# Opening loads in one queue, more idle products in the first norm, no GpSimd arithmetic, and handed-on rows in a spread layout

## The chip, the cores and the metric

The kernel runs on one core of a Trainium2 chip. The metric is the device time of one execution in microseconds, the median of several runs. Three runs of the kernel before gave 3027.7, 3023.4 and 3025.57 us, so its time is 3025.57 us.

A core has these engines: TensorE (PE; its weight loads are shown apart as PEld), VectorE (DVE), ScalarE (ACT), GpSimd (POOL) and SyncE (SP, which here only issues transfers). Sixteen DMA engines move the data between memory and the core's buffers.

## The reference, cut to what matters

The program is one step of a decoder trunk with two layers, for a prompt of 256 tokens and a sample group of 8 sequences of 4 tokens, with 2048 features, all in float32. Each layer does, in this order:

```
x = x + mixer(rmsnorm(x));  x = x + convffn(rmsnorm(x))
x = x + sigmoid(rmsnorm(x) @ Wg) * (p @ Wp)
```

The mixer of layer 0 is causal pooling in four groups of 512 features, with windows w of 2, 4, 8 and 16 tokens: `d = mean(h over the last w tokens) - h`, then `d @ pool_w[group]`, times a scale. For the sample group the window reaches back into `state_pool`, the last 15 normalised rows of each sequence. The mixer of layer 1 is retention.

What the change touches, besides the opening of layer 0, are two of the outputs: the new pooling states. For the prompt they are the last 15 normalised rows (`h[241:256]`); for each sample sequence, the old rows 4 to 14 and the four new normalised rows.

## The kernel before, in words

All large products have 288 moving columns: 256 prompt tokens and 32 sample tokens, features on the partitions. A product in float32 precision is made of three products of split operands (`three`, lines 265 to 267: high by high, low by high, high by low). The weights come in pieces of 256 rows by 512 columns. For each piece, `dma` (line 1396) loads it on SP's queue into one of five buffers (`RAW_BUFS`), `split_hi` (line 1402) rounds it on ACT, and `split_lo` (line 1410) subtracts on DVE. A piece is used by 24 products. Pieces are split two ahead of their use, and the load of piece i+5 is issued when piece i's buffer has been read by `split_lo`.

The order of every engine's instructions is written out by the program itself: the product stream is emitted tile by tile, and between two tiles (`tick`) single operations from two lists, `main` and `side`, are emitted when an estimate of the engines' clocks says that their inputs are there. An engine executes its own instructions in the order of emission.

The opening (`PoolPhase`) has this order:

- `loads` issues the transfers. On SP's queue: the two halves of `x0` (prompt tokens 0 to 127) and of `x1` (128 to 255), with the identity and the four parts of `x4` (the sample's rows in a layout of four times 32 partitions) between them, then `pc`, `gbc`, `sb`, `pq`, and the first five weight pieces. On POOL's queue: `prow` (the norm weights, five loads), `sbb` (state rows for window 16) and a second copy of `gbc` for 32 other partitions.
- `start` squares the tokens' features on ACT (lines 403 and 405), transposes x to features on partitions on PE (`xT`, line 262), and works out the factor of the norm, one number per token (`rms_r`, a chain of twelve tiny DVE operations). While that runs, PE makes eight products of ones by ones, whose result is not used (line 422). In float32 each of these is two instructions.
- The pooling itself is a product: `x0`, `x1` and `sb` are the weights and small matrices `pq` and `pc` are the moving operand, which hold the window's shares. `weigh` (lines 470 and 471) multiplies `pq` by the token's norm factor, and `sbg` (line 476) multiplies the sample's rows by the norm weight. `quad` makes the four feature tiles of a group: three or four products each in a PSUM bank (lines 487 to 494; line 489 adds what the first 128 tokens give to the next ones, 2 to 16 columns wide), then `high` on ACT (498, 499) and `low` on DVE (502, 504). There are three such PSUM banks.
- `start` makes quads 0 and 1 before the first weight piece; quad 2 stands before group 1's pieces (each group has two), quad 3 before group 2's.
- `last` makes the handed-on rows with GpSimd arithmetic on 32 partitions by 2048 features: lines 513 and 514 for the prompt, line 516 for the sample, and three transfers from POOL's queue. Its place in the program is before group 2, but POOL starts each operation as soon as its inputs are there.

`FfnPhase.start` then opens the next phase.

## Time and profile before

| What | Value |
|---|---|
| Median of three runs | 3025.57 us (3023.4 to 3027.7) |
| Span of the profiled execution, first to last instruction | 3020.6 us |
| PE busy | 2998.1 us (99%) |
| DVE busy | 1963.7 us (65%) |
| ACT busy | 1416.2 us (47%) |
| POOL busy | 96.0 us (3%) |
| HBM traffic | 178 GB/s over the span |

The profile gives the profiled execution by its span of 3020.6 us alone. What lies around the span is not shown; the median of the three runs is 4.97 us above it. Start times in the rows are microseconds from the start of the span. `PE mm` is a product into one of the five large PSUM tiles, `PE ms` one into one of the three small ones.

### The profile page before, as it was taken

How to read it: one execution, taken by the hardware profiler on the slowest of the kernel's cores; microseconds unless marked ns; L12 is line 12 of the kernel's file. 1: busy time of each engine (PE TensorE's matmuls, PEld its weight loads, DVE VectorE, ACT ScalarE, POOL GpSimd, SP SyncE). 2: the span in 40 equal slices, each digit the busy share in tenths (PEclk: the TensorE clock that was granted, in tenths of full speed). 3: DMA queues.
4: the chain of work that ended last, by engine and by line, in shares of the span. 5: the costliest groups of instructions: out<-in, count | busy, mean ns of one | idle time of the engine just before them, and what ended most of it. 6: DMA issues, size and time to landing. Idle time of an engine off the chain costs nothing.

```text
span 3020.6 us, 54260 instructions
## 1 busy us (share of the span) xinstructions
PE 2998.1 (99%) x22019; PEld 2945.6 (98%) x22019; DVE 1963.7 (65%) x3396; ACT 1416.2 (47%) x2144; POOL 96.0 (3%) x131
## 2 busy tenths in 40 slices
PE   8999999999999999999999999999999999999998
PEld 8999999999999999999999999999999999999998
DVE  6666756565656767766766767676666565656565
ACT  4544434343444555445444444455444343434454
POOL 3000000000000000000000000000000000000000
PEclk8999999999999999999999999999999999999999
DMA  5655555555555566765766657566555555555543
GB/s 173 176 167 163 165 168 161 168 164 167 166 174 163 167 201 218 238 209 180 237 196 219 221 176 233 191 199 182 163 167 162 167 165 167 164 168 161 178 158 116
DMA packets 287906, 541.81 MB, mean 179 GB/s; under 512 B 18553, under 2 KB 55001, under 8 KB 287465
## 3 DMA queue, kind: packets, MB, share of 16 engines
q1 hardware_dynamic: 274968, 495.44, 53.5%
q0 software_dynamic: 12688, 42.91, 4.2%
q8 instruction: 173, 2.83, 0.4%
q14 instruction: 77, 0.63, 0.1%
HBM read 496.15 MB, written 42.84 MB: 178 GB/s over the span
## 4 chain that ended last, share of the span: by engine, by line
PE 98%; DVE 0%; DMA 0%; ACT 0%; issue 0%; SPq 0%; ACTq 0%
PE mm L265 31%; PE mm L267 30%; PE mm L266 30%; PE ms L262 1%; PE ms L1241 1%; PE ms L1225 1%; PE ms L1242 1%; PE ms L266 0%; PE ms L267 0%; PE ms L265 0%; DMA x<-in_x_prompt 0%; PE ms L1057 0%; PE ms L487 0%; PE ms L491 0%; PE ms L488 0%
## 5 line engine op out<-in xcount | busy, mean ns | idle before, releaser
L1402 ACT CAST hi<-raw 128x1024 fp32r<-128x1024 f32 x864 | 907.1, 1050 | 1393.0 <-PE mm L266 1185.1
L265 PE MATMUL mm<-xh,hi 128*128 128x288 f32 x4928 | 1465.2, 297 | 0.1
L266 PE MATMUL mm<-xl,hi 128*128 128x288 f32 x4928 | 1454.5, 295 | 0.0
L267 PE MATMUL mm<-xh,lo 128*128 128x288 f32 x4928 | 1449.7, 294 | 0.0
L1410 DVE TENSOR_TENSOR lo<-raw,hi 128x1024 fp32r<-128x1024 f32 x864 | 1054.4, 1221 | 552.0 <-ACT hi L1402 550.3
L265 PEld LDWEIGHTS mm<-xh,hi 128*128 128x128 f32 x4928 | 924.5, 188 | 12.1 <-DVE x L532 0.3
L266 PEld LDWEIGHTS mm<-xl,hi 128*128 128x128 f32 x4928 | 925.9, 188 | 4.7
L267 PEld LDWEIGHTS mm<-xh,lo 128*128 128x128 f32 x4928 | 928.4, 188 | 0.0
L266 PE MATMUL mm<-hl,hi 128*128 128x288 f32 x1408 | 415.4, 295 | 0.0
L267 PE MATMUL mm<-hh,lo 128*128 128x288 f32 x1408 | 415.1, 295 | 0.0
L265 PE MATMUL mm<-hh,hi 128*128 128x288 f32 x1408 | 413.3, 294 | 0.0
L265 PEld LDWEIGHTS mm<-hh,hi 128*128 128x128 f32 x1408 | 264.7, 188 | 0.0
L266 PEld LDWEIGHTS mm<-hl,hi 128*128 128x128 f32 x1408 | 264.7, 188 | 0.0
L267 PEld LDWEIGHTS mm<-hh,lo 128*128 128x128 f32 x1408 | 264.5, 188 | 0.0
L632 DVE SCALAR_TENSOR_TENSOR c<-U,cv,c 128x304 f32<-128x304 f32 x352 | 179.4, 529 | 3.5 <-ACT c L629 0.4
L265 PE MATMUL mm<-rhh,hi 128*128 128x288 f32 x512 | 152.2, 297 | 0.0
L267 PE MATMUL mm<-rhh,lo 128*128 128x288 f32 x512 | 151.5, 296 | 0.0
L266 PE MATMUL mm<-rhl,hi 128*128 128x288 f32 x512 | 149.8, 293 | 0.4 <-DVE rhl L1319 0.4
L722 DVE TENSOR_TENSOR x<-x,mm 128x288 f32<-128x288 f32 x192 | 82.5, 450 | 86.5 <-PE mm L267 86.5
L604 DVE TENSOR_TENSOR U<-mm,rb 128x256 f32<-128x256 f32 x176 | 73.7, 419 | 94.8 <-PE mm L267 94.8
L629 ACT ACTIVATE c<-U,cv 128x304 f32<-128x304 f32 x176 | 107.6, 635 | 15.4 <-DVE U L605 15.4
L1229 DVE SCALAR_TENSOR_TENSOR S<-S,ms 128x512 f32<-128x512 f32 x128 | 87.0, 681 | 37.0 <-PE ms L1225 36.8
(265 smaller groups left out, 2154.9 us busy)
## 6 DMA issues: line engine op xcount, KB each, us to landing
raw<-in_ffn_w_up SPq DMA_DIRECT2D x352, 512.0 KB
raw<-in_ffn_w_down SPq DMA_DIRECT2D x176, 512.0 KB
raw<-in_ret_w_in SPq DMA_DIRECT2D x128, 512.0 KB
raw<-in_ple_w_gate SPq DMA_DIRECT2D x64, 512.0 KB
raw<-in_ret_w_in SPq DMA_DIRECT2D x128, 256.0 KB
S<-in_state_ret SPq DMA_DIRECT2D x64, 512.0 KB
out_ret_s<-S POOLq DMA_DIRECT2D x64, 512.0 KB, 4.2
raw<-in_ret_w_out SPq DMA_DIRECT2D x64, 512.0 KB
```

The source lines that it names most:

```text
L262: T.transpose(out, in_, ident[:rows, :rows])
L265: T.matmul(out, w[0], a[0], start=start, stop=False)
L266: T.matmul(out, w[0], a[1], start=False, stop=False)
L267: T.matmul(out, w[1], a[0], start=False, stop=stop)
L604: V.tensor_tensor(U[:, s, 2:258], ps[:, 0:256], rb[:, 0:256], MUL)
L629: A.activation(c[0][:, 0:304], u[:, 2:306], AF.Identity, bias=w(3), scale=w(2))
L632: V.scalar_tensor_tensor(c[0][:, 0:304], u[:, s:304 + s], w(s), c[0][:, 0:304], MUL, ADD)
L722: V.tensor_tensor(x[:, M], x[:, M], ps[:, :NT], ADD)
L1225: T.matmul(ps, st["km", b][:, 128 * kk:128 * kk + 128], self.vst, start=True, stop=True)
L1229: V.scalar_tensor_tensor(s[:, kk], s[:, kk], g ** 4, st["u", b, kk], MUL, ADD)
L1402: A.copy(h, raw[i])
L1410: V.tensor_tensor(l, r, h.bitcast(F32), SUB)
```

## The change

1. Loads: `x1`'s first half is issued right behind `x0`'s second, then the four parts of `x4` and `pc`, then `x1`'s second half. Behind it come `pq` of group 0, `sb`, `gbc`, and the state rows of group 0 alone (112 KB instead of 336 KB), then the rest, two weight pieces, `pq` of groups 2 and 3, `sbb`, and three weight pieces. `sbb` and `gbc` leave POOL's queue (the second copy of `gbc` is gone); `prow` stays there. After the fifth piece, 21 small loads are added on SP's queue: a selection matrix `sel`, and the rows `xe`, `ge`, `g4` for point 4.
2. Norm: the transposed first half of `x1` is copied on DVE instead of ACT, the chain of tiny DVE operations is emitted ahead of the last two transposes, 16 idle products instead of 8, and the copy of the sample's x moves behind the first `sbg`.
3. Pooling products: `pq` is 272 columns per group instead of 384. The product with `x0` is 144 columns wide and reaches 16 columns into the second 128 tokens; the product with `x1` adds to them. The narrow product of line 489 is gone. In group 3 the product with `sb` has 88 rows instead of 32, the added ones with zeros.
4. Handed-on rows: no GpSimd arithmetic. Two products with `sel` spread the norm factors over partitions, one DVE copy keeps them, two DVE operations make the rows (the prompt's 15 rows on 120 partitions by 256 features, the sample's on 128 by 512), and six transfers leave from POOL's queue. They are emitted from `main`, from group 1 on. `FfnPhase.start` waits in the program's order until they are emitted.

```diff
-    pq = np.zeros((128, 4, 384), f)
+    pq = np.zeros((128, 4, 272), f)
...
+    sel = np.zeros((128, 2, 128), f)
+    sel[:32, 0] = np.tile(np.eye(32), (1, 4))
+    for t in range(15):
+        sel[113 + t, 1, 8 * t:8 * t + 8] = 1
...
             for i, t in enumerate((self.x0, self.x1)):
                 for h in range(2):
                     c = slice(h * (D // 2), (h + 1) * (D // 2))
+                    if i == h == 1:
+                        for j in range(4):
+                            SP.dma_start(self.x4[32 * j:32 * j + 32], x4[j])
+                        SP.dma_start(self.pc, I["pc"])
                     SP.dma_start(t[:, c], xp[128 * i:128 * i + 128, c])
                     if i == h == 0:
                         SP.dma_start(ident, I["ident"])
-                    if i + h == 1:
-                        for j in range(2 * i, 2 * i + 2):
-                            SP.dma_start(self.x4[32 * j:32 * j + 32], x4[j])
-            SP.dma_start(self.pc, I["pc"])
-            SP.dma_start(self.gbc[0:32], g0.partition_broadcast(32))
-            SP.dma_start(self.sb[0:32], I["x_sample"].rearrange("b t d -> (b t) d"))
-            SP.dma_start(self.pq[:, 0], I["pq"][:, 0])
-            SP.dma_start(self.sb[32:88, 0:1536], I["state_pool"][0, :, 8:15, 0:1536])
...
+            SP.dma_start(self.pq[:, 0], I["pq"][:, 0])
+            SP.dma_start(self.sb[0:32], I["x_sample"].rearrange("b t d -> (b t) d"))
+            SP.dma_start(self.gbc, g0.partition_broadcast(32))
+            SP.dma_start(self.sb[32:88, 0:512], I["state_pool"][0, :, 8:15, 0:512])
             SP.dma_start(self.pq[:, 1], I["pq"][:, 1])
-            dma(0)
+            SP.dma_start(self.sb[32:88, 512:2048], I["state_pool"][0, :, 8:15, 512:2048])
+            for i in range(2):
+                dma(i)
             SP.dma_start(self.pq[:, 2:4], I["pq"][:, 2:4])
-            for i in range(1, RAW_BUFS):
+            SP.dma_start(self.sbb, I["state_pool"][0, :, :, 1536:2048])
+            for i in range(2, RAW_BUFS):
                 dma(i)
-            GP.dma_start(self.sbb, I["state_pool"][0, :, :, 1536:2048])
-            GP.dma_start(self.gbc[96:128], g0.partition_broadcast(32))
+            SP.dma_start(self.sel, I["sel"])
+            SP.dma_start(self.xe, xp[241:256].rearrange("t (e c) -> (t e) c", e=8))
+            for t in range(15):
+                SP.dma_start(self.ge[8 * t:8 * t + 8], g0.rearrange("(e c) -> e c", e=8))
+            for j in range(4):
+                SP.dma_start(self.g4[32 * j:32 * j + 32], g0[512 * j:512 * j + 512].partition_broadcast(32))
...
-            self.xT(1, 0, False)
-            self.xT(1, 1, False)
+            self.xT(1, 0, True)
+            self.xT(1, 1, True)
...
+            V.tensor_tensor(ssq[:, 0:1], tiny[:, 9:10], tiny[:, 10:11], ADD)
+            V.tensor_copy(ssq[:32, 2:3], ps[:32, 0:1])
+            V.tensor_tensor(ssq[:, 1:2], tiny[:, 11:12], tiny[:, 12:13], ADD)
+            release(ps)
+            rms_r()
             self.xT(1, 2, False)
             self.xT(1, 3, False)
...
-            for _ in range(8):
+            for _ in range(16):
                 T.matmul(pw[:, 0:128], ones, ones, start=True, stop=True)
...
             self.direct(self.sbg(0))
+            A.copy(x[:, :, 256:288].rearrange("p (c j) t -> p c j t", j=4),
+                   px.rearrange("p (j c t) -> p c j t", j=4, c=4))
...
-                    T.matmul(ps[:, 0:128], self.x0[:, c], self.pq[:, gi, 0:128], start=True, stop=True)
-                    T.matmul(ps[:, 128:256], self.x1[:, c], self.pq[:, gi, 256:384], start=True, stop=False)
-                    T.matmul(ps[:, 128:128 + w], self.x0[:, c], self.pq[:, gi, 128:128 + w], start=False, stop=True)
+                    T.matmul(ps[:, 0:144], self.x0[:, c], self.pq[:, gi, 0:144], start=True, stop=True)
+                    T.matmul(ps[:, 128:256], self.x1[:, c], self.pq[:, gi, 144:272], start=False, stop=True,
+                             skip_group_check=True)
...
-                chains.append([op_(860 if gi < 3 else 1070, prod, nb=1), Op("A", 480, high), Op("V", 440, low)])
+                chains.append([op_(700 if gi < 3 else 850, prod, nb=1), Op("A", 480, high), Op("V", 440, low)])
...
         def last(self):
-            r = slice(96, 128)
-            GP.tensor_scalar(self.sqs[r], self.x1[r], rtok[r, 1:2], None, MUL)
-            GP.tensor_tensor(self.sqs[r], self.sqs[r], self.gbc[r], MUL)
-            GP.dma_start(O["pool_p"][0, 0], self.sqs[113:128])
-            GP.tensor_scalar(self.sb[0:32], self.sb[0:32], rtok[:32, 2:3], None, MUL)
-            GP.dma_start(O["pool_s"][0, :, 11:15, :], self.sb[0:32])
-            GP.dma_start(O["pool_s"][0, :, 0:11, :], I["state_pool"][0, :, 4:15, :])
+            c = {}
+            def factors():
+                ps = c[0] = sbank()
+                T.matmul(ps[:, 0:1], self.sel[:, 0], rtok[:, 2:3], start=True, stop=True)
+                T.matmul(ps[:, 1:2], self.sel[:, 1], rtok[:, 1:2], start=True, stop=True)
+            def keep():
+                V.tensor_copy(self.rsel, c[0][:, 0:2])
+                release(c[0])
+            def rows():
+                V.scalar_tensor_tensor(self.xe, self.xe, self.rsel[:120, 1:2], self.ge, MUL, MUL)
+                V.scalar_tensor_tensor(self.x4, self.x4, self.rsel[:, 0:1], self.g4, MUL, MUL)
+            def out():
+                GP.dma_start(O["pool_p"][0, 0].rearrange("t (e c) -> (t e) c", e=8), self.xe)
+                for j in range(4):
+                    GP.dma_start(O["pool_s"][0, :, 11:15, 512 * j:512 * j + 512], self.x4[32 * j:32 * j + 32])
+                GP.dma_start(O["pool_s"][0, :, 0:11, :], I["state_pool"][0, :, 4:15, :])
+                ready.add("rows")
+            main.extend(chained([op_(250, factors, nb=1), Op("V", 150, keep), Op("V", 900, rows)]) + [Op("N", 0, out)])
...
-                    if gi == 2:
+                    if gi == 1:
                         self.last()
...
-            force(lambda: not side)
+            force(lambda: not side and "rows" in ready)
```

## Rows read from the trace of the kernel before

**Rows 1.** Stretches: length, busy us (instructions) by engine, PE clock, DMA share, GB/s.

```profile
24.00:31.00 7.00, 5.74 (x27) 5.64 (x27) 5.70 (x7) 3.55 (x10) 6.24 (x3) 0.50 0.50 192
...
46.00:60.00 14.00, 14.00 (x113) 13.80 (x113) 10.79 (x27) 7.96 (x22) 0.00 (x0) 1.00 0.39 114
...
80.00:1000.00 920.00, 920.00 (x6920) 918.77 (x6919) 574.61 (x978) 420.23 (x601) 5.41 (x10) 1.00 0.56 167
```

**Rows 2.** Chain that ended last, in order of time: start, length, what.

```profile
4.81 10.77 DMA x<-in_x_prompt
...
19.88 4.06 DVE sb L476
...
26.33 0.59 PE ms L487 x2
...
38.00 0.40 PE mm L265
...
46.56 0.30 PE ms L487 x2
46.87 0.22 PE ms L488 x2
47.09 0.12 PE ms L489 x2
47.22 0.24 PE ms L491 x2
```

**Rows 3.** Waits of PE, first 60 us: total, times, longest.

```profile
PE ms L491 <- DVE sb L476: 2.2, 1, 2.2
...
PE ms L487 <- ACT xh L499: 1.3, 1, 1.3
```

**Rows 4.** Timeline of DVE and POOL: start, length, engine, line, operation.

```profile
19.56 5.57 POOL L513 TENSOR_SCALAR sqs<-x,rtok 32x2048 f32<-32x2048 f32 x1 [14.59 <-ACT x L429]
19.81 4.12 DVE L476 TENSOR_TENSOR sb<-sb,gbc 32x512 f32<-32x512 f32 x1
...
25.21 4.52 POOL L514 TENSOR_TENSOR sqs<-sqs,gbc 32x2048 f32<-32x2048 f32 x1
...
25.80 4.01 DVE L471 TENSOR_SCALAR pq<-pq,rtok 128x128 f32<-128x128 f32 x1
...
29.73 0.67 DVE L476 TENSOR_TENSOR sb<-sb,gbc 32x512 f32<-32x512 f32 x1
```

**Rows 5.** DMA: traffic of 2 to 16 us by queue; then stretches as in rows 1.

```profile
DMA packets 1455, 3.60 MB, mean 257 GB/s; under 512 B 300, under 2 KB 671, under 8 KB 1366
...
q0 software_dynamic: 288, 0.57, 17.7%
...
2.00:6.00 4.00, 1.03 (x5) 1.07 (x6) 0.00 (x0) 1.17 (x3) 2.97 (x6) 1.00 0.87 294
...
10.00:13.00 3.00, 1.97 (x8) 1.56 (x8) 0.56 (x2) 1.15 (x2) 0.00 (x0) 1.00 0.98 203
```

**Rows 6.** Timeline of PE: the idle products of line 422.

```profile
18.34 2.86 PE L422 MATMUL ms<-ones 128*128 128x128 f32 x16
```

**Rows 7.** Last stretches of PE alone: length, busy us (instructions), clock, DMA share, GB/s.

```profile
3006.80:3007.20 0.40, 0.40 (x4) 0.65 0.00 0
```

**Rows 8.** Groups by line, 22 to 45 us: count, busy us, mean ns of one.

```profile
L1410 DVE TENSOR_TENSOR lo<-raw,hi 128x1024 fp32r<-128x1024 f32 x4 | 4.9, 1214 | 0.0
...
L502 DVE SCALAR_TENSOR_TENSOR xl<-ms,par,xh 128x256 fp32r<-128x256 f32 x8 | 3.8, 476 | 4.1 <-ACT xh L499 4.1
...
L1402 ACT CAST hi<-raw 128x1024 fp32r<-128x1024 f32 x4 | 4.2, 1052 | 2.6 <-issue 2.6
...
L498 ACT ACTIVATE xh<-ms,par 128x256 fp32r<-128x256 f32 x8 | 3.8, 474 | 11.8 <-PE ms L491 11.8
```

**Rows 9.** Waits of SP's queue, first 60 us.

```profile
SPq L1396 <- DVE lo L1410: 32.5, 6, 12.1
...
SPq L392 <- DMA x<-in_x_prompt: 2.2, 1, 2.2
```

More of the change, by code (lines that the diff above doesn't have):

```diff
@@ L55, in _constants @@
             for j in range(max(0, t - win + 1), t + 1):
-                pq[j % 128, w, t + 128 * (j // 128)] += share
-            pq[t % 128, w, t + 128 * (t // 128)] -= 1
+                pq[j % 128, w, t + 16 * (j // 128)] += share
+            pq[t % 128, w, t + 16 * (t // 128)] -= 1
         for b in range(8):
@@ L70, in _constants @@
     c["pq"], c["pc"] = pq, pc
+    sel = np.zeros((128, 2, 128), f)
+    sel[:32, 0] = np.tile(np.eye(32), (1, 4))
+    for t in range(15):
+        sel[113 + t, 1, 8 * t:8 * t + 8] = 1
+    c["sel"] = sel
     half = DK // 2
@@ L367, in loads @@
             self.sb, self.sbb = t("sb", [128, D]), t("sbb", [120, 512])
-            self.pq, self.pc = t("pq", [128, 4, 384]), t("pc", [128, 6, 32])
-            self.prow, self.gbc, self.sqs = t("prow", [128, 128]), t("gbc", [128, D]), t("sqs", [128, D])
+            self.pq, self.pc = t("pq", [128, 4, 272]), t("pc", [128, 6, 32])
+            self.prow, self.gbc, self.sqs = t("prow", [128, 128]), t("gbc", [32, D]), t("sqs", [128, D // 2])
+            self.sel, self.rsel = t("sel", [128, 2, 128]), t("rsel", [128, 2])
+            self.xe, self.ge, self.g4 = t("xe", [120, 256]), t("ge", [120, 256]), t("g4", [128, 512])
             g0 = I["norm_mix"][0]
@@ L420, in start @@
             pw = sbank()
-            for _ in range(8):
+            for _ in range(16):
                 T.matmul(pw[:, 0:128], ones, ones, start=True, stop=True)
             release(pw)
-            V.tensor_tensor(ssq[:, 0:1], tiny[:, 9:10], tiny[:, 10:11], ADD)
-            V.tensor_copy(ssq[:32, 2:3], ps[:32, 0:1])
-            release(ps)
-            V.tensor_tensor(ssq[:, 1:2], tiny[:, 11:12], tiny[:, 12:13], ADD)
-            rms_r()
-            A.copy(x[:, :, 256:288].rearrange("p (c j) t -> p c j t", j=4),
-                   px.rearrange("p (j c t) -> p c j t", j=4, c=4))
             A.copy(par, pp[:, 0:128])
@@ L469, in weigh @@
             self.rdy = [
-                oa(256, lambda: A.activation(w[:, 0:256], w[:, 0:256], AF.Copy, scale=rtok[:, 0:1]), 1),
-                ov(128, lambda: V.tensor_scalar(w[:, 256:384], w[:, 256:384], rtok[:, 1:2], None, MUL))]
+                oa(144, lambda: A.activation(w[:, 0:144], w[:, 0:144], AF.Copy, scale=rtok[:, 0:1]), 1),
+                ov(128, lambda: V.tensor_scalar(w[:, 144:272], w[:, 144:272], rtok[:, 1:2], None, MUL))]
             return list(self.rdy)
@@ L485, in prod @@
                     ps = d[0] = sbank()
-                    w = WINDOWS[gi]
-                    T.matmul(ps[:, 0:128], self.x0[:, c], self.pq[:, gi, 0:128], start=True, stop=True)
-                    T.matmul(ps[:, 128:256], self.x1[:, c], self.pq[:, gi, 256:384], start=True, stop=False)
-                    T.matmul(ps[:, 128:128 + w], self.x0[:, c], self.pq[:, gi, 128:128 + w], start=False, stop=True)
+                    T.matmul(ps[:, 0:144], self.x0[:, c], self.pq[:, gi, 0:144], start=True, stop=True)
+                    T.matmul(ps[:, 128:256], self.x1[:, c], self.pq[:, gi, 144:272], start=False, stop=True,
+                             skip_group_check=True)
                     if gi < 3:
@@ L492, in prod @@
                     else:
-                        T.matmul(ps[:, 256:288], self.sb[:32, c], self.pc[:32, 3], start=True, stop=False)
+                        T.matmul(ps[:, 256:288], self.sb[:88, c], self.pc[:88, 3], start=True, stop=False)
                         T.matmul(ps[:, 256:288], self.sbb[:, 128 * (M - 12):128 * (M - 11)], self.pc[:120, 4],
```

## The prediction

> **What bounds the kernel now.** I read the table of stretches first. Once the work is under way TensorE is never idle: 920.00 us busy of the 920 from 80 to 1000 us [rows 1]. Whatever the change does to VectorE, ScalarE or GpSimd there costs nothing, and a microsecond is worth a microsecond only where TensorE waits or runs slowly. That is the opening, so I read the chain of waits over the first 60 us next. It shows three things [rows 2]. First, the second half of x1 is waited for from 4.81 to 15.58 us. Second, squares and the norm's chain take until 19.88, and there the sample's rows (line 476) hold the path for 4.06 us. Third, the pooling products follow, and the first weight product starts only at 38.00. The table of waits names the two holes that VectorE leaves in TensorE: 2.2 us before line 491 and 1.3 us before a line 487 [rows 3]. The timeline says why [rows 4]. The VectorE operation of line 476 that takes 4.12 us from 19.81 ran beside GpSimd's line 513 (19.56 to 25.13) and takes 0.67 us at 29.73. Line 471 took 4.01 us beside line 514 (25.21 to 29.73).
>
> The granted clock belongs to this. It is 0.50 (1.2 GHz) all through 24 to 31 us and 1.00 (2.4 GHz) from 46 to 60 [rows 1]. It had fallen after TensorE stood still for the 2.2 us, and a line 487 costs 0.59 us at the one level and 0.30 at the other [rows 2]. So the hole of 2.2 us costs far more than itself.
>
> A measurement of this kernel tells 0.2%, about 6 us, from no change. Times below are in the profiled execution, whose span is 3020.6 us. The median is 4.97 us above that span, and I carry this difference over unchanged.
>
> **The change part by part.** *Arrival of x1's second half (T).* Before it was 15.58 [rows 2]. Ahead of it the new order has 2.10 MB of x, 0.07 of identity, 0.26 of x4, 0.10 of pc and, on the other queue, 0.07 of prow. The x loads run at 294 GB/s as from 2 to 6 us, the small ones at 203 as from 10 to 13 [rows 5]: 2.17/0.294 = 7.4 us and 0.43/0.203 = 2.1 us, from a first byte at about 2.1, which gives 11.6. But loads issued later get ahead on some of the sixteen engines: before, 3.60 MB had landed by 16 us [rows 5], where 2.42 MB of SP's queue and 0.57 of the other stood up to x1, so 0.6 MB. With a third to a half of that, 0.8 us more, I take T = 12.4. Bounds: 11.6, and 15.6 if the order buys nothing.
>
> One rule of the Trainium skill bears here ("DMA: Bandwidth & Descriptors", Issuing engines are not separate DMA queues): transfers share the same sixteen engines and interleave, whichever engine issued them, and issuing from several only saves issue time. The trace agrees so far as the other queue's 0.57 MB held 17.7% of the DMA time of 2 to 16 us [rows 5]. By that rule taking them out of the way moves T, as here. If the queues did not disturb each other, only the order on SP would count, and T would stay close to 15.6.
>
> *From T to the first pooling product (S).* The norm needs what it needed: 19.88 - 15.58 = 4.3 us, then 0.67 for line 476 without GpSimd beside it [rows 2, 4], so T+5.0. What line 476 reads lands behind x1: pq 0.14, sb 0.26, gbc 0.26 and 0.11 MB of state at 203 GB/s make 3.8 us, T+3.8, in time by half a microsecond. The idle products end later. TensorE has, from T, eight transposes and that of prow, each 0.21 us at half clock (twice the 0.11 that one instruction of a line 488 pair takes at full clock [rows 2]): T+1.9. Then 32 idle instructions instead of 16. The first 16 took 2.7 us, from 18.34 to the next product at 21.04 [rows 6]; between 16 x 0.21 = 3.4 and 16 x 0.11 = 1.7, so the clock rose among them. The next 16 at full clock add 1.7: T+6.3. All at half clock they end at T+8.7; at full clock from the start, at T+5.4. So the doubled idle products, not the norm, set S = T+6.3 = 18.7. They cost 1.3 us over the T+5.0 and buy the clock.
>
> *Quads 0 and 1, up to the first weight product.* Line 489 goes (0.12 us a tile), line 487 grows from 128 to 144 columns (0.03): a tile is 0.30+0.22+0.12+0.24 = 0.88 at full clock before [rows 2] and 0.79 after. Eight of them are 6.3 us, the lower bound. But each needs a high of 0.47 and a cast of 0.18 on ScalarE and as much on VectorE, three banks go round, and on these engines lie hi (1.05 each), lo (1.21 each) [rows 8], line 471 and another line 476. Followed through: first low done at S+2.0, then lines 471 and 476 to S+2.9, three more lows with ScalarE's hi between them to S+5.3, lo to S+6.5, the fifth low S+7.1, the eighth tile S+7.9. So the first weight product stands at S+8.0 = 26.7 instead of 38.00: 11.3 us. The upper bound is eight tiles at half clock, S+12.6. The weight piece must be there for hi at S+3.1 = 21.8; it is 1.0 MB behind the state rows, at most 4.9 us after T+3.8, 21.1.
>
> *Twelve weight products* ran at half clock from 38.00 to 40.80; at full clock they take 12 x 0.133 = 1.6. Gain 1.2.
>
> *Quads 2 and 3* ran at full clock with TensorE never idle (46 to 60 us [rows 1]): eight tiles save 0.09 each, 0.7; four one-column instructions with sel at 0.06, as half a line 489, take 0.25 back. Gain 0.5.
>
> *At nothing:* the three VectorE operations for the rows (bounded by two lows and a line 476, 0.2 to 1.7 us), since VectorE is busy 10.79 of 14.00 us there [rows 1]; six transfers from GpSimd's queue instead of three, which nobody waits for; two copies of x1 on VectorE, which waits for x1 then; the copy of the sample's x behind line 476, under the first product. The 21 small loads stand ahead of the sixth weight piece on SP. Past the eighth, a load is issued when the one eight places earlier has landed (the 17th waited 2.2 us for x1, the 9th [rows 9]). So thirteen of them are issued after the fifth piece has landed at about 26, at 0.33 to 0.54 us each: until 32. Before, the sixth piece waited for its buffer, up to 12.1 us [rows 9], until 33. It is wanted on ScalarE at 39 and on TensorE at 49, and lands by 36. The lower planned cost of a tile (700 for 860) only shifts the estimate.
>
> Sum: 11.3 + 1.2 + 0.5 = 13.0 us. Span 3007.6, median 3012.6 us. Late next are the idle products and then ScalarE and VectorE in the two quads.
>
> **The rivals.** *A: x1 arrives no earlier.* The DMA engines are at 0.98 in 10 to 13 us [rows 5], so an order only shuffles. Against it: 0.57 MB of the other queue and later loads stand aside. T = 15.6, S = 21.9, first weight product 29.9: gain 8.1 + 1.2 + 0.5, time 3015.8.
>
> *B: the clock falls again in the quads.* For it: line 476 is in time by half a microsecond only, and near the end the clock falls (0.65 on the way to 0.50) while TensorE is busy 0.40 of 0.40 us with one-column products [rows 7], so being busy is not enough. Against it: quads 2 and 3 at full clock keep it (1.00 over 46 to 60 [rows 1]). If gbc lands at T+8.5, two us after the idle products' end, S is 21.6 and eight tiles at half clock end at 34.2: gain 3.8 + 0.5, time 3021.3. It decides from a hole as long as the old one, 2.2 us; a fall without a hole, after half of the tiles, costs about 3 plus the 1.2, time 3017.
>
> *C: slower, through SP's queue.* The small loads hold up the sixth weight piece. For it: thirteen serial issues, each tied to a landing. Against: issues of 0.33 to 0.54 us. TensorE loses from the point where the piece lands after 46.7 (49 less hi and lo); to lose the 13.0 it must land at 60, each of the thirteen taking 2.4 us. At 3 us each they end at 65 and it lands at 68: 21 lost, time 3034.
>
> *D: the idle products see an earlier rise and T is 11.6:* S = 17.0, time 3010.9, inside the forecast's own range.
>
> **How the numbers follow.** Forecast with D 0.66, A 0.13, B 0.13, C 0.04, and 0.04 for a shift in the later order that opens small holes, time near 3026. Faster by over 0.2% (below 3019.5) are the forecast, A and a third of B, 0.84; same 0.11 (the rest of B, and half of the last); slower 0.05. The forecast's own range is 3009 to 3016, from T 11.6 to 14 and the idle products' bounds; to hold 8 of 10 with A and the milder B, 3008.5 to 3018.5.
>
> **What would show it.** Line 476 at 0.67 us and no operation of GpSimd on data; x1's last half at 11.6 to 14; the granted clock at 1.00 from within the idle products on; the first weight product at 25 to 29 us; TensorE without a hole after it. I am wrong if the first weight product starts later than 33, if the clock shows 0.50 after the idle products, or if TensorE waits for a weight piece between 40 and 60 us.

## The result and the profile after

Four runs of the changed kernel gave 3006.09, 3005.87, 3009.77 and 3009.78 us, median 3007.93. Four of the kernel before gave a median of 3024.87 (3023.4 to 3027.7). The ratio is 0.9943, 95% interval 0.9929 to 0.9957: faster by 16.9 us. The forecast was 3012.6, and the median lies 0.6 us under the low end of its range, 3008.5. With the later runs there are 19 executions of this same kernel: median 3009.77, from 3004.95 to 3014.16. The kernel before has 40, median 3024.8. So the changed kernel scatters more widely than its first four runs showed, and that scatter is a subject of its own below.

The profiled execution took 3006.09 us, with a span of 3004.2 against 3020.6. First the table of stretches, two of those in [rows 1] (columns as there).

```profile
24.00:31.00 7.00, 7.00 (x55) 7.00 (x54) 6.19 (x13) 3.73 (x7) 0.00 (x0) 1.00 0.28 92
46.00:60.00 14.00, 14.00 (x107) 14.00 (x106) 12.57 (x23) 7.45 (x12) 7.76 (x14) 1.00 0.70 194
```

The first row is the change: from 24 to 31 us the granted clock is 1.00 where it was 0.50, and TensorE is busy 7.00 of 7.00 us instead of 5.74. From 80 to 1000 us TensorE is busy 920.00 us, as before.

The chain of waits in order of time (start, length, what) tells how it gets there.

```profile
1.66 6.72 DMA x<-in_x_prompt
8.43 4.08 PE mm L268 x20
...
13.79 3.57 PE ms L444 x32
17.36 0.25 PE ms L504 x2
...
24.57 0.22 PE mm L271
...
31.66 0.33 PE ms L504 x2
31.99 0.22 PE ms L505 x2
32.21 0.14 PE ms L508 x2
...
41.10 0.33 PE ms L504 x2
41.43 0.22 PE ms L505 x2
41.65 0.14 PE ms L510 x2
41.79 0.22 PE ms L511 x2
```

Read against [rows 2]: the wait for x ends at 8.38 on this chain, and from 8.43 TensorE itself sets the pace, with its transposes and then with the 32 instructions of the idle products. As these end, the first pooling product starts, at 17.36. The first weight product stands at 24.57, where it was 38.00. A tile of quad 2 is 0.33 + 0.22 + 0.14 = 0.69 us, a tile of quad 3 0.33 + 0.22 + 0.14 + 0.22 = 0.91.

The timeline of VectorE (start, length, line, operation) has the operation that took 4.12 us beside GpSimd in [rows 4], now without it.

```profile
16.62 0.67 DVE L493 TENSOR_TENSOR sb<-sb,gbc 32x512 f32<-32x512 f32 x1
```

From 12 to 60 us the largest time that TensorE's products wait in the table of waits (total, times, longest) is this; the 2.2 us of [rows 3] are gone.

```profile
PE ms L504 <- DVE xl L521: 0.7, 1, 0.7
```

The two operations that make the handed-on rows, in the groups of VectorE from 24 to 60 us (count, busy us, mean ns, idle before):

```profile
L543 DVE SCALAR_TENSOR_TENSOR x<-x,rsel,g 128x512 f32<-128x512 f32 x1 | 0.7, 748 | 0.0
L542 DVE SCALAR_TENSOR_TENSOR xe<-xe,rsel,ge 120x256 f32<-120x256 f32 x1 | 0.5, 480 | 0.0
```

With the copy of the factors (0.2 us) they take 1.4 us of VectorE from 46 us on, where TensorE is never idle: they cost nothing, as forecast.

Where the 16.4 us of span came from, by product starts in the two profiles (the tables below use the same starts, which can lie 0.2 us ahead of the chain's):

| Until | Before | After | Gain in this part |
|---|---|---|---|
| first weight product | 37.81 | 24.41 | 13.40 |
| twelve weight products later | 40.80 | 26.09 | 1.31 |
| the products after quad 2 | 49.08 | 33.63 | 0.74 |
| the products after quad 3 | 60.78 | 43.68 | 1.65 |
| end of the span | 3020.6 | 3004.2 | -0.7 |

### The profile page after: what moved, and what is told of

It is laid out like the page before. It is cut to its first block, busy times and chain, and to the rows that moved or that the text cites. A ratio compares the mean times of both kernels' runs of the same rounds, so it can differ in the third digit from the quotient of the medians.

```text
span 3004.2 us, 54263 instructions
## 1 busy us (share of the span) xinstructions
PE 2985.6 (99%) x22007; PEld 2934.2 (98%) x22007; DVE 1957.9 (65%) x3401; ACT 1415.4 (47%) x2142; POOL 80.7 (3%) x129
## 4 chain that ended last, share of the span: by engine, by line
PE 98%; DMA 1%; DVE 0%; ACT 0%; issue 0%; SPq 0%; ACTq 0%; DVEq 0%
PE mm L271 31%; PE mm L273 30%; PE mm L272 30%; PE ms L268 1%; PE ms L1274 1%; PE ms L1258 1%; PE ms L1275 1%; PE ms L272 0%; PE ms L271 0%; PE ms L273 0%; DMA raw<-in_ret_w_in 0%; PE ms L1090 0%; DMA x<-in_x_prompt 0%; DVE lo L1443 0%; PE mm L268 0%
## 5 line engine op out<-in xcount | busy, mean ns | idle before, releaser
L1435 ACT CAST hi<-raw 128x1024 fp32r<-128x1024 f32 x864 | 907.5, 1050 | 1391.0 <-PE mm L272 1190.8
```

The source lines that it names most:

```text
L1435: A.copy(h, raw[i])
```

## The experiments

Runs of one group shared a chip and its runs of the kernel before, whose medians were 3023.96, 3024.0, 3024.21 and 3025.41 us. Each row is one profiled execution: T is when ScalarE starts to square x1's last half, S the first pooling product, W the first weight product, Q the products after quad 3; all in us. "Fall" is the last moment up to W, or at it, at which the granted clock falls to 0.50 (in e7_rows32 0.2 us behind W). The median and its range are over all timed executions of that label.

| Run | T | S | W | Q | Fall | Span | Median of runs (range) |
|---|---|---|---|---|---|---|---|
| before | 15.66 | 21.04 | 37.81 | 60.78 | 23.67 | 3020.6 | 3024.87 (3023.4 to 3027.7) |
| after | 12.47 | 17.20 | 24.41 | 43.68 | none | 3004.2 | 3007.93 (3005.87 to 3009.78) |
| e1_same | 14.33 | 20.97 | 28.18 | 47.45 | none | 3008.7 | 3011.28 (3006.42 to 3013.18) |
| e10_same2 | 15.15 | 19.79 | 27.60 | 46.86 | none | 3007.8 | 3009.67 (3005.15 to 3012.21) |
| e15_same3 | 14.86 | 19.50 | 29.33 | 50.73 | 27.28 | 3011.3 | 3008.59 (3004.95 to 3014.16) |
| e2_gpsimd | 12.44 | 17.54 | 27.61 | 48.91 | none | 3007.9 | 3011.19 (3010.19 to 3013.13) |
| e3_narrow | 12.19 | 17.38 | 25.33 | 46.99 | none | 3008.2 | 3012.34 (3009.41 to 3017.5) |
| e4_hold | 12.82 | 17.45 | 25.54 | 44.81 | none | 3006.0 | 3008.35 (3007.17 to 3011.08) |
| e5_idle8 | 13.09 | 17.32 | 24.81 | 44.09 | none | 3005.6 | 3006.83 (3005.2 to 3007.33) |
| e6_order | 13.32 | 20.44 | 27.64 | 46.92 | none | 3008.3 | 3009.46 (3008.51 to 3011.75) |
| e7_rows32 | 15.36 | 21.62 | 29.54 | 51.54 | 29.76 | 3013.6 | 3015.41 (one run) |
| e8_before_rows | 13.86 | 19.12 | 27.76 | 49.87 | none | 3009.5 | 3015.26 (3011.3 to 3019.08) |
| e9_warm | 11.80 | 16.83 | 26.11 | 47.12 | 23.22 | 3010.6 | 3009.63 (3009.27 to 3012.39) |
| e11_idle8 | 14.32 | 18.55 | 28.91 | 50.06 | 26.32 | 3014.2 | 3010.82 (3006.72 to 3015.94) |
| e12_idle0 | 12.80 | 17.02 | 26.85 | 46.11 | 15.67 | 3006.4 | 3008.74 (3007.56 to 3010.97) |
| e13_split | 14.93 | 19.56 | 26.78 | 46.05 | none | 3007.4 | 3008.26 (3006.99 to 3009.25) |
| e14_split_idle8 | 12.00 | 16.22 | 23.73 | 43.00 | none | 3003.9 | 3008.08 (3005.67 to 3010.1) |

### GpSimd's arithmetic put back: e2_gpsimd

```diff
-            main.extend(chained([op_(250, factors, nb=1), Op("V", 150, keep), Op("V", 900, rows)]) + [Op("N", 0, out)])
...
+            GP.tensor_scalar(self.sqs[r], self.x1[r], rtok[r, 1:2], None, MUL)
+            GP.tensor_tensor(self.sqs[r], self.sqs[r], self.gbc[r], MUL)
...
```

> The change without its point 4: the handed-on rows are again made by GpSimd arithmetic (lines 513 to 516 of before). Theory (GpSimd's operations hold VectorE up, and the hole this makes lets the clock fall): line 476's multiplication takes about 4 us instead of 0.67, TensorE stands still for 2 to 3.5 us before the first pooling product, the clock is at 0.50 in the quads, and the first weight product comes 8 to 11 us later, span 3012 to 3016. Rival (the 16 idle products and the earlier data now cover it): VectorE's delay costs at most its own 3.4 us, span up to 3008, and the clock stays at 1.00.

The ratio was 0.9956 (0.9944 to 0.9969). The timelines of GpSimd and of VectorE, one fence each:

```profile
16.34 5.57 POOL L518 TENSOR_SCALAR sqs<-x,rtok 32x2048 f32<-32x2048 f32 x1 [12.40 <-DVE rtok L254]
27.50 5.44 POOL L519 TENSOR_TENSOR sqs<-sqs,gbc 32x2048 f32<-32x2048 f32 x1 [5.60 <-DMA gbc<-in_norm_mix]
```

```profile
16.59 4.12 DVE L481 TENSOR_TENSOR sb<-sb,gbc 32x512 f32<-32x512 f32 x1
...
29.36 3.67 DVE L476 TENSOR_SCALAR pq<-pq,rtok 128x128 f32<-128x128 f32 x1
32.95 0.67 DVE L481 TENSOR_TENSOR sb<-sb,gbc 32x512 f32<-32x512 f32 x1
```

Both long VectorE operations begin while a GpSimd operation runs, and the same operation at 32.95, as it ends, takes 0.67 us. By the Trainium skill ("SBUF — State Buffer", SBUF: two separate sides) a GpSimd operation that reads the buffer and a VectorE operation with two inputs in it, or in a two-port mode, take one shared pair of ports: whichever starts first keeps it for the whole instruction, and the other is blocked. The trace agrees in kind, 4.12 us against 0.67. In length it does not quite: the first long operation ends at 20.71, 1.2 us before GpSimd's is shown to end.

TensorE's wait in this run and the granted clock across it (the two views in this order):

```profile
PE ms L496 <- DVE sb L481: 2.6, 1, 2.6
```

```profile
18.00:21.00 3.00, 0.41 (x4) 0.24 (x3) 2.71 (x1) 0.00 (x0) 3.00 (x1) 1.00 1.06 375
21.00:28.00 7.00, 5.81 (x47) 5.54 (x47) 5.71 (x16) 5.83 (x18) 1.40 (x2) 1.00 0.74 253
```

The hole came back, 2.6 us, longer than the 2.2 before. The clock did not fall after it: the column before the DMA share stays at 1.00. So the arithmetic costs W 3.2 us and Q 5.2 (48.91 for 43.68; in quad 2 TensorE waits another 1.9, behind the operation of 3.67) by waiting alone, and 3.7 in the span, where this version has neither the products with `sel` nor the wait near 1040 us told below; this rests on two profiles whose T agree (12.44 and 12.47). The medians don't show it: e1_same, the changed kernel in the same group of runs, had 3011.28. That a hole of this size brings the clock down, as the prediction said, holds in the kernel before and not here: a hole can start a fall and need not.

### The handed-on rows alone, in the kernel before: e8_before_rows

```diff
-            GP.tensor_scalar(self.sqs[r], self.x1[r], rtok[r, 1:2], None, MUL)
-            GP.tensor_tensor(self.sqs[r], self.sqs[r], self.gbc[r], MUL)
...
+                V.scalar_tensor_tensor(self.xe, self.xe, self.rsel[:120, 1:2], self.ge, MUL, MUL)
+                V.scalar_tensor_tensor(self.x4, self.x4, self.rsel[:, 0:1], self.g4, MUL, MUL)
```

> The kernel before with point 4 alone: handed-on rows without GpSimd arithmetic. Theory (GpSimd's two holes cost TensorE's clock, and with them gone the quads run at full clock): line 476 takes 0.67 us, the first weight product comes at 28 to 30 us instead of 37.8, the granted clock stays at 1.00 after its rise, span 3010 to 3012. Rival (GpSimd costs what its holes last, as putting it back into the changed kernel suggested, where the first weight product came 3.2 us later and the clock stayed up): 3.2 to 5.2 us, span 3015 to 3018.

Point 4 of the change with the old loads (but for `gbc`'s second copy), norm and products gave 0.9972 (0.996 to 0.9983), some 8.7 us: about half of the whole gain. The multiplication of the sample's rows takes 0.67 us there, with no GpSimd operation beside it. In the profile, the fastest of its six executions, W comes 10.05 us earlier, and the clock stays up through the quads. But T is 1.8 us earlier too, and `gbc`'s second copy (0.26 MB on GpSimd's queue) went with the arithmetic, so not all of this is the arithmetic's. That it gains more than e2_gpsimd's 3.7 because here the fall of the clock goes with the hole fits this profile; what the slower executions did is not shown. Quads 2 and 3 stay as they were: from W to Q 22.1 us, of which the changed kernel needs 19.3.

### The pooling products in their old form: e3_narrow

```diff
-                    T.matmul(ps[:, 0:144], self.x0[:, c], self.pq[:, gi, 0:144], start=True, stop=True)
-                    T.matmul(ps[:, 128:256], self.x1[:, c], self.pq[:, gi, 144:272], start=False, stop=True,
-                             skip_group_check=True)
...
+                    T.matmul(ps[:, 0:128], self.x0[:, c], self.pq[:, gi, 0:128], start=True, stop=True)
+                    T.matmul(ps[:, 128:256], self.x1[:, c], self.pq[:, gi, 256:384], start=True, stop=False)
+                    T.matmul(ps[:, 128:128 + w], self.x0[:, c], self.pq[:, gi, 128:128 + w], start=False, stop=True)
...
-                        T.matmul(ps[:, 256:288], self.sb[:88, c], self.pc[:88, 3], start=True, stop=False)
+                        T.matmul(ps[:, 256:288], self.sb[:32, c], self.pc[:32, 3], start=True, stop=False)
```

> The change without its point 3: pq is 384 columns wide again, the narrow product is back, and group 3 multiplies 32 rows. Theory (a narrow product costs its own time and that of the weight load behind it, which a wide product would have hidden): tiles cost 0.88 us again instead of 0.69 in quad 2 and 1.33 instead of 0.91 in quad 3, which is 2.4 us over the two, and the first two quads, paced by ScalarE and VectorE, lose 0.5 to 1.6 more: 3 to 4 us in all. Rival, as I had priced it (0.09 a tile): 0.7 us over quads 2 and 3 and 0 to 0.7 before, 0.7 to 1.5 in all.

The ratio was 0.996 (0.9948 to 0.9973), 1.1 us above e1_same of the same group and not separable from it. The profile separates them: with T 0.3 earlier, Q is 3.3 later than after the change, 2.4 of it from W on. One tile of quad 2 and one of quad 3 in the chain of this run:

```profile
33.67 0.30 PE ms L505 x2
33.97 0.22 PE ms L506 x2
34.20 0.12 PE ms L507 x2
34.32 0.24 PE ms L509 x2
```

```profile
44.50 0.30 PE ms L505 x2
44.80 0.22 PE ms L506 x2
45.03 0.13 PE ms L507 x2
45.16 0.33 PE ms L511 x2
45.49 0.34 PE ms L512 x2
```

They last 0.89 and 1.33 us, against 0.69 and 0.91 in the changed kernel. Set side by side with its chain above, the narrow product's own 0.12 is only part of it. The sample's product behind it takes 0.24, and 0.14 once it stands behind a product of 128 columns: 0.10 more. Line 504, with 16 columns more, gives back 0.03. So 0.19 or 0.20 a tile. In quad 3 the rest is in lines 511 and 512, 0.67 for 0.36.

### 32 rows instead of 88: e7_rows32

```diff
-                        T.matmul(ps[:, 256:288], self.sb[:88, c], self.pc[:88, 3], start=True, stop=False)
+                        T.matmul(ps[:, 256:288], self.sb[:32, c], self.pc[:32, 3], start=True, stop=False)
```

> The changed kernel with 32 instead of 88 rows in group 3's product with sb, as before, the zeros left out. Theory (a weight load of other rows than the product before cannot be hidden, so products of 128, 32 and 120 rows in turn cost more than of 128, 88 and 120): a tile of quad 3 takes 1.1 to 1.2 us instead of 0.91, quad 3 0.8 to 1.1 us more. Rival (the price of quad 3 before was the narrow product's alone): 0.91 us a tile still.

One tile of quad 3 in its chain:

```profile
48.04 0.33 PE ms L504 x2
48.37 0.22 PE ms L505 x2
48.59 0.33 PE ms L510 x2
48.92 0.34 PE ms L511 x2
```

With 32 rows the product takes 0.33 us instead of 0.14, and the next one, whose operands are the same, 0.34 instead of 0.22. So 56 rows of zeros make the tile 0.31 us cheaper. The weight loads fit the theory only in part: with 32 rows the load starts with its product, at 48.52, and with 88 rows 0.10 us ahead of it (41.38 and 41.48 after the change), though 88 is another number than the 128 before it. The run's time says nothing here (one run, x1 late, and a fall of the clock at 29.76); the tile does.

### The unchanged kernel again: e1_same, e10_same2, e15_same3

> The changed kernel itself, unaltered, to see its spread: two of its four executions so far had a span of 3004 us and two of 3008. Theory (the clock falls for a few microseconds in quads 0 and 1 in some executions, since the products there leave TensorE partly idle): the spans lie in groups, one near 3004 and one near 3008, and the slower group has the lower mean granted clock, by the 3 to 7 us at half clock that a fall costs. Rival (the spread comes from small holes anywhere, as in the kernel before): the spans fill 3004 to 3008 evenly, with one mean clock.

> The changed kernel once more, unaltered, beside the one with 8 idle products. Theory (x1's arrival, 12.5 and 14.3 us in the two executions looked at, and the moment of the clock's rise, 11.9 and 18.6 us, differ from execution to execution): spans again between 3004 and 3012, median of all executions near 3009.8. Rival (the first four executions, median 3007.9, are the rule): median 3006 to 3008.

> The changed kernel, unaltered, as the measure for the other two: median 3009 to 3011, two groups, if the theory of differing executions holds; a median of 3006 to 3008 would say that the slower group was a matter of the chip.

The same program spread over 9.2 us of time, and its four profiles differ in four things. First T: 12.47, 14.33, 15.15 and 14.86 with one order of loads. Second, the moment at which the clock first rises. Before its first record, the clock column reads 1.00 whatever the products do, so their lengths show it. TensorE's timeline after the change, and then that of e1_same:

```profile
12.59 1.09 PE L268 MATMUL mm<-ident,x 128*128 128x128 f32 x8
...
13.62 3.74 PE L444 MATMUL ms<-ones 128*128 128x128 f32 x32
```

```profile
14.39 1.94 PE L268 MATMUL mm<-ident,x 128*128 128x128 f32 x8 [0.64 <-DMA x<-in_x_prompt]
...
16.33 4.80 PE L444 MATMUL ms<-ones 128*128 128x128 f32 x32
```

In the first, the transposes of x1's last half already run at 2.4 GHz (eight in 1.09 us), and so do all idle products behind them, which end at S: T+4.7. In e1_same those transposes run at 1.2 GHz (1.94), the clock rises among the idle products, and S is T+6.6. What TensorE did before does not tell the cases apart: ahead of x1's last half it transposed for 4.53 us from 9.02 in e1_same and for 4.53 us from 8.87 in e15_same3, where the last eight then took 1.07.

Third, a fall in quads 0 and 1. The stretches of e15_same3, and then of e10_same2, whose T is nearly the same:

```profile
19.00:26.00 7.00, 5.00 (x42) 4.76 (x41) 3.31 (x11) 4.17 (x14) 0.00 (x0) 1.00 1.05 284
27.00:34.00 7.00, 6.25 (x28) 6.14 (x28) 5.63 (x13) 2.90 (x9) 0.00 (x0) 0.52 0.38 129
```

```profile
19.00:26.00 7.00, 6.03 (x51) 5.79 (x49) 4.70 (x14) 5.54 (x16) 0.00 (x0) 1.00 1.05 301
27.00:34.00 7.00, 7.00 (x54) 7.00 (x55) 6.20 (x13) 3.72 (x7) 0.00 (x0) 1.00 0.29 97
```

From 19 to 26 us, ahead of the fall at 27.28, TensorE is busy for 5.00 us in e15_same3 and for 6.03 in e10_same2. Q is 3.9 us later and the span 3.5 longer. Its waits and the chain name what is late:

```profile
PE ms L504 <- DVE xl L521: 2.7, 2, 1.9
...
ACT hi L1435 <- DMA raw<-in_pool_w: 2.2, 2, 1.9
```

```profile
13.53 10.64 DMA raw<-in_pool_w
...
26.22 1.22 DVE lo L1443
...
27.98 0.84 PE ms L504 x2
```

The first weight piece is issued at 13.5, no later than in the other three profiles (13.0 to 13.8), but lands only at 24.17. ScalarE's `hi` waits 1.9 us for it (0.5 in e10_same2); VectorE's `lo` follows at 26.22; the last low of the quads stands behind it, and TensorE behind that.

Fourth, and not in the opening: near 1040 us TensorE waits for VectorE, for 0.5 us in the profile after, and for 0.8, 1.0 and 0.2 in e1_same, e10_same2 and e15_same3. The profile after has this line between 1000 and 1070 us; the one before has no wait there.

```profile
PE ms L321 <- DVE acc L316: 0.5, 1, 0.5
```

In e9_warm and e11_idle8, variants below, this wait is 1.9 and 2.3 us, and the granted clock behind it is 0.50 (1044 to 1047 and 1047 to 1050 us). So part of the scatter of their times lies outside the opening. Why VectorE is late there is not shown.

### Fewer bytes ahead of the weight piece: e13_split, e14_split_idle8

```diff
-            SP.dma_start(self.sb[0:32], I["x_sample"].rearrange("b t d -> (b t) d"))
-            SP.dma_start(self.gbc, g0.partition_broadcast(32))
...
+            SP.dma_start(self.sb[0:32, 0:1024], xs[:, 0:1024])
+            SP.dma_start(self.gbc[:, 0:1024], g0[0:1024].partition_broadcast(32))
...
-            SP.dma_start(self.sb[32:88, 512:2048], I["state_pool"][0, :, 8:15, 512:2048])
+            SP.dma_start(self.sb[32:88, 512:1024], st[:, :, 512:1024])
...
```

> The changed kernel with 0.49 MB less ahead of the first weight piece: of sb and gbc only the first 1024 columns, of the state rows only those of groups 0 and 1; the rest behind the second piece. Theory (the late piece makes the holes in the quads in which the clock falls): ScalarE no longer waits for the first piece, the clock stays up in the quads, and the slower group of executions thins out, median 1 to 3 us below the changed kernel's. Rival (the groups are x1's arrival): the same median within 1 us, with the same spread.

> As e13_split, with 8 idle products instead of 16. Theory (idle products are on the path when the clock rises late, and the clock's fall in the quads came from the late piece, not from having fewer of them): median 1 to 2 us below e13_split's. Rival (fewer idle products leave a hole in which the clock falls in some executions): the same or 1 to 4 us above it.

The ratios are 0.9943 (0.993 to 0.9955) and, with eight idle products as well, 0.9941 (0.9928 to 0.9953): not distinguishable from the changed kernel. The profiles say that the edit did its work: before W ScalarE waits for no piece in either (1.4 and 2.4 us of such waits come behind W), and in neither did the clock fall. e13_split has nearly the T and the S of e15_same3. ScalarE takes up the first piece in e15_same3, and then in e13_split, as follows:

```profile
24.19 1.04 ACT L1435 CAST hi<-raw 128x1024 fp32r<-128x1024 f32 x1 [1.89 <-DMA raw<-in_pool_w]
```

```profile
22.25 1.07 ACT L1439 CAST hi<-raw 128x1024 fp32r<-128x1024 f32 x1
```

W is 2.6 us earlier in e13_split and Q 4.7. In this pair of profiles the late piece and the fall go together. e13_split spread over 2.3 us in five runs, e15_same3 over 9.2 on the same chip. That would fit fewer falls; five runs don't show it, and the medians, 3008.26 and 3008.59, are the same.

### Idle products: e5_idle8, e11_idle8, e12_idle0, e4_hold, e9_warm

```diff
-            for _ in range(16):
+            for _ in range(8):
                 T.matmul(pw[:, 0:128], ones, ones, start=True, stop=True)
```

> The changed kernel with 8 idle products instead of 16 (line 444). Theory (the norm, not the idle products, sets the first pooling product once the clock has risen early; the added ones only keep the clock): they end 1.7 us earlier, TensorE stands still for 1 to 2 us before the first pooling product, which starts at the same distance of 4.7 to 5.0 us from the arrival of x1's last half; if the clock falls in that hole, the tiles take twice as long and the span grows by 5 to 7 us, otherwise the time is the same. Rival (the idle products are on the path, as the forecast had it): the first product comes 1.3 to 1.7 us earlier and so does the end.

> The changed kernel with 8 idle products, once more. Theory (when the clock rises only among the idle products, they are on the path, so fewer of them start the pooling products up to 1.7 us earlier; the clock did not fall in the hole that they leave): median 1.5 to 3 us below the unaltered kernel's, spans 3003 to 3008. Rival (its first four executions had early clocks by chance): the same median as the unaltered kernel's within 1 us, or executions at 3010 and more in which the clock fell in the hole.

> The changed kernel without any idle product. Theory (some are needed, since TensorE would stand still for about 3 us while the norm is worked out, longer than the 2.2 us in the kernel before after which the clock fell): the clock falls or rises only with the weight products, the eight tiles take twice as long in all or most executions, span 3009 to 3014. Rival (no idle products are needed at all, as 8 for 16 suggested): 3003 to 3008.

e5_idle8 and e11_idle8 are one kernel: nine executions with a median of 3007.33, from 3005.2 to 3015.94. The first ratio, 0.994 (0.9923 to 0.9956), looked like a gain, the second, 0.9954 (0.9942 to 0.9966), took it back. Fewer idle products do bring S nearer to T: TensorE then waits for the scaled `pq`, and S is T+4.2 in both profiles, where the sixteen end at T+4.6 to T+4.7 with the clock up. The wait in e5_idle8:

```profile
PE ms L504 <- ACT pq L487: 1.2, 1, 1.2
```

With none the ratio is 0.9947 (0.9933 to 0.996). In that run TensorE waited longer for `pq` and then ran the quads at half clock:

```profile
PE ms L502 <- ACT pq L485: 3.0, 1, 3.0
```

```profile
16.00:25.00 9.00, 7.98 (x36) 7.98 (x37) 5.72 (x18) 5.31 (x15) 0.00 (x0) 0.50 1.04 346
```

W came 9.8 us after S instead of 7.2: 2.6 us for nearly all of quads 0 and 1 at 1.2 GHz.

e4_hold puts six idle products into two holes of the quads, e9_warm puts 21 between the transposes:

```diff
+                for _ in range({11: 2, 20: 4}.get(n, 0)):
+                    T.matmul(pi[:, 0:128], ones, ones, start=True, stop=True)
```

```diff
+            warm(10)
             for q in range(4):
                 self.xT(0, q, True)
+                if q % 2:
+                    warm(3)
...
+            warm(5)
```

> The changed kernel with idle products (ones by ones) put into the two holes that TensorE has within quads 0 and 1: two before the fifth tile (hole of 0.52 us) and four before the eighth (0.86 us). Theory (the slower executions are those in which the clock falls in these quads): all spans lie at 3004 to 3005, none at 3008, so the median falls by about 2 us. Rival (the spread has nothing to do with the clock in the quads): the same mixture of 3004 and 3008, or up to 0.5 us more for products that do not quite fit the holes.

> The changed kernel with idle products also ahead of the norm: ten before the first transposes, while TensorE waits for x, three behind x0's first and second half each, and five behind the transposes of x4 (21 products of ones by ones in all). Theory (the executions differ by the moment at which the clock rises and by x1's arrival; only the first can be governed): the clock rises before 9 us in every execution, the transposes of x1 and the 16 idle products run at full clock, the first pooling product stands at 4.7 to 5.0 us from x1's arrival instead of 4.7 to 6.7, median 1 to 2 us lower than the changed kernel's, spread from x1's arrival alone. Rival (the added products push the transposes back): first pooling product 0.5 to 1.5 us later than that.

e4_hold: 0.9948 (0.9934 to 0.9962). W is 8.1 us after S instead of 7.2, and the spread of its runs, 3.9 us, is just that of the first four of the changed kernel. So the spread stayed, against my theory that falls in the quads alone make it; only one of the five executions was profiled. e9_warm: 0.9953 (0.9938 to 0.9967). The clock was up from 6.15 on and S came at 16.83, early. Then ScalarE waited 1.3 us for the weight piece, TensorE 1.4 for VectorE, and the clock was down from 23.22 to 30.04. Here the early rise gained nothing, as the piece came late.

### The old order of loads: e6_order

```diff
-                    if i == h == 1:
-                        for j in range(4):
-                            SP.dma_start(self.x4[32 * j:32 * j + 32], x4[j])
-                        SP.dma_start(self.pc, I["pc"])
...
+            GP.dma_start(self.sbb, I["state_pool"][0, :, :, 1536:2048])
```

> The change without its point 1: the loads in the order of before (sbb from GpSimd's queue, all state rows at once, gbc and sb ahead of pq), with the new small loads behind them and the second copy of gbc still gone. Theory (the order brings x1's last half 1.5 to 3 us earlier): its arrival is at 14.5 to 16 us and all that follows is later by as much, span 3006 to 3011 where the changed kernel's execution with the early clock had 3004.2. Rival (the gain is from having fewer bytes on the way, not from their order): arrival at 12 to 13.5, no difference beyond 1 us.

The ratio was 0.9951 (0.9936 to 0.9966), and T 13.32, inside the 12.47 to 15.15 of the new order (15.36 in e7_rows32). The order is not shown to bring x1 forward. What the old order lacks here is `gbc`'s second copy on GpSimd's queue; e8_before_rows, also without it, has T 13.86, and the kernel before, with it, 15.66 in its one profile. That points to bytes and not to order, but one profile of before can't settle it.

## Why the prediction was right, and where it failed

*GpSimd beside VectorE.* Right: 0.67 us for 4.12, and shown from both sides by e2_gpsimd and e8_before_rows. The price of the hole "through the clock" was a matter of chance that I wrote as a rule: e2_gpsimd has the hole and no fall.

*T = 12.4.* The profile has 12.47, and this was luck. The other three of the same kernel have 14.3 to 15.2. In the profiled execution T was not even on the path: TensorE transposes from 8.43 on without waiting for x. My bounds, 11.6 and 15.6, hold all four; the cause that I gave, order, is not shown by e6_order. The rest of that argument holds in its size: GpSimd's queue carries 0.07 MB and 1.8% of the DMA time in 2 to 16 us, where it had 0.57 MB and 17.7% [rows 5].

```profile
q0 software_dynamic: 160, 0.07, 1.8%
```

By the Trainium skill ("DMA: Bandwidth & Descriptors", Issuing engines are not separate DMA queues) transfers interleave on the same sixteen engines, whichever engine issued them. By that rule T should come earlier without those bytes; the four T's and e6_order neither show nor refute it, since a scatter of 2.7 us lies over it.

*S = T+6.3, set by the idle products.* In all four profiles the idle products do set S. The size is right in e1_same (T+6.6) and 1.6 too large in the profiled execution and in e10_same2 and e15_same3 (T+4.6 to 4.7), where the clock had risen before the idle products began. My lower bound for that case, T+5.4, still had the nine transposes behind T at half clock, at 1.9 us; the idle products begin at T+1.1 there. The norm would have allowed T+4.2 (e5_idle8, e11_idle8), not T+5.0. Over that the sixteen cost 0.4 to 0.5 us with an early clock and 2.4 with a late one.

*First weight product at S+8.0.* It came 7.2 us after S in the profile and in e1_same, 7.8 in e10_same2. With T and S: 24.4 to 28.2 without a fall, 29.3 with one, round the forecast 26.7. This large term was right on the average of the four (27.4) and too late for the first profiled, by 2.1 us.

*Twelve weight products.* Forecast 1.2, measured 1.3.

*Quads 2 and 3: "Gain 0.5".* This is the step that failed, in every profile: the term was mis-sized. I priced the narrow product at its own 0.12, took nothing from the ones beside it, and so had 0.7 for the eight tiles. Measured were 0.74 and 1.65, together 2.4. Two things were missing. The product after a narrow one is longer by 0.10: the rows had its 0.24 (line 491 behind line 489 [rows 2]), but no row had it behind a wide one, and I took it as fixed. And I did not look at quad 3 at all: the 56 rows of zeros, told in the change as an addition, save 0.31 of the 0.42 us a tile (e7_rows32). After quad 3 the four profiles of the changed kernel give back 0.7 to 1.4 us. The products with `sel`, forecast at 0.25, set the weight products 0.36 us back and the one behind them takes 0.22 instead of 0.13: the same mistake at a smaller size. The wait near 1040 us takes 0.2 to 1.0; the rest stays open.

*The sum.* Against the profiled span of 3004.2 the forecast span of 3007.6 is 3.4 too high: 2.1 from the first weight product, 0.1 from the twelve, 1.9 from the quads, less the 0.7 given back. The difference of 4.97 us that I carried from span to median adds 1.2, since it is 3.73 here. It was no constant: in nearly every later run the time is 1.7 to 2.0 us above that run's own span, so by that some 3 of the 4.97 were only how far the profiled execution ran ahead of the median one. With the 1.9 in the sum the range's low end would have stood at 3006.6, under the median. Over all 19 executions the median, 3009.77, lies inside the range as forecast: which executions the first four were had a part in the miss.

*The rivals.* A (x1 no earlier) is in part what happens in e10_same2: T 15.15, and there 3007.8 of span, as the quads and the clock pay all the same. The milder B came true in e15_same3, and likewise in e7_rows32, e9_warm and e11_idle8; against e10_same2 it cost 3.5 to 3.9 us. In all four ScalarE waited for the first weight piece (0.6 to 2.1 us), which I had put at T+8.7 and in time for S+3.1. With S at T+4.2 to T+5.0, as in three of them, that is no longer in time, and in e15_same3 it landed at 24.17, T+9.3. That the piece causes the fall is supported, not proved: with fewer bytes ahead of it, in two runs, it came in time and the clock stayed up; but the clock also stayed up in e10_same2 and e4_hold, where ScalarE waited 0.5 and 0.8 us. C did not show: TensorE waits for no weight piece between 40 and 60 us. D's earlier rise is what the profile after shows, without its T of 11.6.

*What stays open.* Why the same loads bring x1 at 12.5 in one execution and at 15.2 in another, and when a late piece brings the clock down: in e4_hold ScalarE waited 0.8 us and the clock stayed up, in e7_rows32 it waited 0.6 and the clock fell. No version tried is shown to be faster than the changed kernel.

## What to carry to other kernels

Price a small product by the whole tile with and without it, since the next product's time changes with it; and where a product has far fewer rows than its neighbours, try padding them with zeros (here 88 for 32). Where an opening is bound by transfers, profile the same kernel several times before crediting a change of order: T scattered here by as much as the change was to move it. Take GpSimd arithmetic off the path of VectorE first; about half of this gain came with it and with the 0.26 MB that it no longer needed.

## What the runs showed of the hardware that was not expected

- A product on 32 rows between products of 128 and 120 rows takes 0.33 us and makes the next 0.34; on 88 rows they take 0.14 and 0.22.
- TensorE can stand 2.6 us (e2_gpsimd) and keep a granted clock of 1.00; in e7_rows32 the clock fell at 29.76, after 10.10 us in which TensorE was busy for 8.28 at 1.00.
- The clock rose to 2.4 GHz behind transposes alone: in the profile after, the last eight run in 1.09 us, ahead of any idle product.
